# Down products of an encoder block by Strassen's scheme over pairs of token blocks, their stationary operands made beside the gate and up products; gate by SiLU

## The chip, the cores and the metric

The kernel runs on one core of a Trainium2 chip. The metric is device time in microseconds (us); all times here are of that core. The core has a matrix engine (TensorE, PE in the profile), a vector engine (VectorE, DVE), an activation engine (ScalarE, ACT), a general engine (GpSimd, POOL) and a sequencer that here only issues transfers (SyncE, SP). Each engine works through its own list of instructions in order and waits on semaphores for the others.

## The reference

One layer of an encoder on 2048 tokens of width 1024, in float32: a mixer (gated linear attention in both directions and a gated spatial mixing), then the feed-forward part, which is what matters here:

```python
x = x + concat(y_a, y_b) @ w_out
h2 = rmsnorm(x, norm2_g)
x = x + (silu(h2 @ w_gate) * (h2 @ w_up)) @ w_down    # d_ff = 2816
return rmsnorm(x, final_norm_g)
```

## The kernel before

Everything is kept with channels on the 128 partitions and tokens along the free dimension. The 2048 tokens are four blocks of 512 (`NB`, `TB`); a tile of 128 channels by 512 tokens of a block is the unit of work, 1024 channels are eight such tiles (`KT`), the 2816 channels of the feed-forward part are 22 (`NF`). Each float32 operand is split in two, a high part rounded by ScalarE (a cast) and the rest, by a subtraction on VectorE, and a product is three matmuls of 128x128 by 128x512: high by high, high by low, low by high (`mm_pass3`, L109 to L112).

Before the feed-forward part come the mixer's projections, attention, gating and the product with `w_out`. The normalised inputs of the feed-forward part and the residual wait in DRAM (`d_h`, `d_x`).

**Gate and up** (`seven`, `gate_set`, `up_set`, from L866) already use Strassen's scheme in Winograd's form. A pair of blocks, first (3, 2), then (1, 0), by the two halves of the 1024 input channels is a 2x2 matrix of moving operands, two tiles of output channels by two halves of inputs is the stationary one, and seven products of 12 matmuls stand for the eight. `moving` (L232) makes the seven moving operands of a pair in SBUF (`slots`). `Stationary.job` (L328) makes the seven stationary ones of each set just ahead of their use, on VectorE and ScalarE, from weights loaded on SP, up to four products ahead. For each pair there are 11 sets for gate and 11 for up, taken in the order `STEADY` = 0, 4, 3, 1, 2, 6, 5 within a set. Two products share a bank of PSUM with another: product 4 adds to what product 0 left, and so must wait until ScalarE has copied that out (`u2`); product 6 adds to product 3's after VectorE has read it. A quarter of a gate set then goes through tanh on ScalarE (L946) and a multiply-add on VectorE (L947); a quarter of an up set is multiplied by it (L958) and written to DRAM by POOL (`d_a`, L959).

**Down** (from L983) has no such scheme. The four blocks go one after the other in the order 3, 2, 1, 0. For each of the 22 input tiles the activation is loaded from DRAM (`act_unit`, L1014) and split, 128 rows of `w_down` are loaded (`down_unit`, L1001) and split, and eight products of three matmuls add into eight banks of PSUM. At a block's end the eight results are added to the residual (L1075), squared, summed over the partitions by a matmul with ones, and the block is normalised (`leave`, L1028) and written out by POOL while the next block's products run. Only the last block's last four input tiles are done in two halves of 256 tokens, so that the first half is normalised under the second's matmuls (L1080 to L1128).

The order on every engine comes from the framework's scheduler, which lists instructions by its own estimate of when each can start; buffers in pools (`bufs`) and semaphores decide the rest. Transfers that SP issues go in order too: one that waits holds those behind it.

## Time and profile before

| | us |
|---|---|
| median of 3 runs | 2127.7 (2124.53 to 2128.52) |
| the profiled execution's own time | 2127.53 |
| its span, first to last instruction | 2125.8 |
| mean granted TensorE clock | 0.998 of full speed |
| PE, DVE, ACT, POOL busy | 2088.7, 1362.1, 871.8, 169.3 |
| first gate matmul, first down matmul, last down matmul start | 778.48, 1628.43, 2115.08 |

The profile is of one execution. Busy times say how long an engine had an instruction in work; a matmul is pipelined, so its listed 0.39 us overlaps with the next, which starts 0.227 us later. On VectorE too the listed durations overlap by a little when nothing waits. In the views below a name such as `pd` is a tile (the bank of a down product), `out<-in` says what an instruction writes and reads, and `L110` is a line of the program.

### The profile page before, as it was taken

What the parts mean: (1) busy time and instruction counts of PE and PEld (TensorE: products, weight loads), DVE (VectorE), ACT (ScalarE), POOL (GpSimd) and SP (SyncE); (2) the same over time, 40 slices, a digit from 0 to 9 for tenths busy, and PEclk for the clock granted to TensorE, in tenths of its full rate; (3) what the DMA queues carried; (4) which work ended last, traced back from release to release, by engine and by line L of the source; (5) the groups of instructions that cost most, each with busy time, mean ns of one, the idle gap of its engine ahead of it and who ended that gap; (6) DMA issues with size and microseconds to landing.
All of it is one profiled execution on the core that took longest, in us unless ns stands there. A gap on an engine that the chain in (4) does not pass through costs nothing.

```text
span 2125.8 us, 25829 instructions
## 1 busy us (share of the span) xinstructions
PE 2088.7 (98%) x9728; PEld 1705.8 (80%) x9728; DVE 1362.1 (64%) x2134; ACT 871.8 (41%) x1475; POOL 169.3 (8%) x266
## 2 busy tenths in 40 slices
PE   8999999999999999999999999999999999999998
PEld 6777777888888878888888888888888888888887
DVE  4977666666756768676666976666666455353633
ACT  5855455464635543332332523323324333233321
POOL 0112213011110100000000000000000000000000
PEclk9999999999999999999999999999999999999999
DMA  7543225353553433222212342222225537364531
GB/s 262 199 142 120 98 96 184 133 199 125 170 187 127 169 129 144 84 70 85 95 66 83 126 149 83 69 85 95 79 72 185 185 121 257 128 216 149 180 114 40
DMA packets 94110, 281.42 MB, mean 132 GB/s; under 512 B 11681, under 2 KB 19745, under 8 KB 90785
## 3 DMA queue, kind: packets, MB, share of 16 engines
q1 hardware_dynamic: 79968, 227.33, 31.5%
q0 software_dynamic: 14016, 52.44, 6.7%
q8 instruction: 76, 1.25, 0.2%
q14 instruction: 50, 0.40, 0.1%
HBM read 225.20 MB, written 54.53 MB: 132 GB/s over the span
## 4 chain that ended last, share of the span: by engine, by line
PE 88%; DVE 5%; ACT 3%; DMA 3%; issue 1%; SPq 0%; POOL 0%; DVEq 0%; ACTq 0%; POOLq 0%
PE pd L110 8%; PE pd L111 8%; PE pd L112 8%; PE pout L112 3%; PE pout L111 3%; PE pout L110 3%; PE pu L110 1%; PE pu L111 1%; PE pu L112 1%; PE pz L110 1%; PE pz L111 1%; PE pg L110 1%; PE pg L111 1%; PE pz L112 1%; PE pg L112 1%
## 5 line engine op out<-in xcount | busy, mean ns | idle before, releaser
L959 POOL DMA_DIRECT2D da<-q x88 | 47.6, 541 | 803.1 <-DVE q L958 770.3
L946 ACT ACTIVATE th<-cg 128x512 f32<-128x512 f32 x66 | 41.5, 631 | 107.9 <-DVE cg L944 99.5
L947 DVE SCALAR_TENSOR_TENSOR cg<-th,cg 128x512 f32<-128x512 f32 x66 | 45.3, 688 | 15.6 <-ACT th L946 15.6
L826 DVE TENSOR_TENSOR xc<-pout,xc 128x512 f32<-128x512 f32 x32 | 21.9, 688 | 45.0 <-PE pout L112 44.9
L958 DVE SCALAR_TENSOR_TENSOR q<-q,cg 128x512 f32<-128x512 f32 x66 | 45.3, 687 | 0.6
L541 POOL TENSOR_SCALAR qs<-QK,misc 128x128 f32<-128x128 f32 x30 | 24.9, 833 | 164.5 <-PE po L545 83.6
L1031 POOL DMA_DIRECT2D out_dram<-xg x12 | 8.6, 716 | 368.3 <-DVE xg L1028 368.3
L565 DVE SCALAR_TENSOR_TENSOR sf<-sf,misc,dsb 64x128 f32<-64x128 f32 x56 | 19.8, 354 | 23.9 <-ACT dsb L555 23.2
L731 DVE SCALAR_TENSOR_TENSOR sb<-sb,misc,dsr 128x128 f32<-128x128 f32 x30 | 9.9, 345 | 33.8 <-PE pob L721 33.0
L548 ACT COPY ot<-po 128x256 f32<-128x256 f32 x32 | 10.3, 376 | 46.1 <-issue 23.4
L536 PEld LDWEIGHTS po<-v,s 128*128 128x128 f32 x128 | 15.5, 191 | 16.1 <-issue 13.8
L536 PE MATMUL po<-v,s 128*128 128x128 f32 x128 | 18.1, 284 | 9.9 <-DVE s L513 9.9
L1016 ACT CAST a_8h<-ar 128x512 fp32r<-128x512 f32 x32 | 18.5, 618 | 17.8 <-DMA ar<-da 17.7
L716 POOL TENSOR_SCALAR qb<-qb,misc 128x128 f32<-128x128 f32 x30 | 18.9, 640 | 78.1 <-DMA qb<-dq 66.5
L1103 DVE TENSOR_TENSOR xg<-pd,xg 128x256 f32<-128x256 f32 x16 | 6.8, 424 | 28.2 <-PE pd L112 27.8
L1075 DVE TENSOR_TENSOR xg<-pd,xg 128x512 f32<-128x512 f32 x24 | 16.6, 690 | 12.2 <-PE pd L112 12.2
L1105 ACT ACTIVATE lsq<-xg 128x256 f32<-128x256 f32 x16 | 6.7, 417 | 40.9 <-DVE xg L1103 40.9
L735 ACT ACTIVATE junk<-o 128x128 f32<-128x128 f32 x64 | 19.8, 310 | 8.8 <-DMA o<-do 4.4
L375 ACT ACTIVATE xk<-xk 128x1024 f32<-128x1024 f32 x16 | 17.0, 1063 | 13.8 <-DMA xk<-in_xtok_dram 13.8
L1017 DVE TENSOR_TENSOR a_0l<-ar,a_0h 128x512 fp32r<-128x512 f32 x32 | 20.6, 686 | 1.0 <-ACT a_0h L1016 1.0
L1017 DVE TENSOR_TENSOR a_8l<-ar,a_8h 128x512 fp32r<-128x512 f32 x32 | 20.7, 681 | 0.6 <-ACT a_8h L1016 0.6
L507 PEld LDWEIGHTS sc<-QK 64*128 64x128 f32 x256 | 15.6, 187 | 6.5 <-issue 5.3
(3680 smaller groups left out, 7337.0 us busy)
## 6 DMA issues: line engine op xcount, KB each, us to landing
wdn<-in_wdn_dram SPq DMA_DIRECT2D x88, 512.0 KB, 3.5
da<-q POOLq DMA_DIRECT2D x88, 256.0 KB, 2.3
ar<-da SPq DMA_DIRECT2D x88, 256.0 KB, 4.1
wo<-in_wo_dram SPq DMA_DIRECT2D x32, 512.0 KB, 3.6
wqk<-in_wqk_dram SPq DMA_DIRECT2D x16, 512.0 KB, 3.7
xk<-in_xtok_dram SPq DMA_DIRECT2D x16, 512.0 KB, 5.1
wv<-in_wv_dram SPq DMA_DIRECT2D x16, 512.0 KB, 3.4
xc<-in_xT_dram SPq DMA_DIRECT2D x4, 2048.0 KB, 9.2
```

What stands on the lines that cost most here:

```text
L110: nc.tensor.matmul(out=out, lhsT=whi, rhs=ahi, start=start, stop=False, **kw)
L111: nc.tensor.matmul(out=out, lhsT=whi, rhs=alo, start=False, stop=False, **kw)
L112: nc.tensor.matmul(out=out, lhsT=wlo, rhs=ahi, start=False, stop=stop, **kw)
L536: nc.tensor.matmul(out=po[hd % 2][:, hd // 2, :], lhsT=s[:, hd, :], rhs=vs[t][:, hd, :], start=hd < 2, stop=g == 0 and hd > 1)
L541: nc.gpsimd.tensor_scalar_mul(qs[:, m, :], qd[m][:, c], ech[:, m, 2 * g:2 * g + 1])
L565: nc.vector.scalar_tensor_tensor(out=sn[r, m, :], in0=sf[r, m, :], scalar=dec[r, m, g:g + 1], in1=dsb[r, 2 * m + a, :], op0=ALU.mult, op1= ...
L826: nc.vector.tensor_tensor(out=xt[:, n, :], in0=p, in1=xt[:, n, :], op=ALU.add)
L946: nc.scalar.activation(out=th, in_=a, func=AF.Tanh, scale=0.5)
L947: later.append(lambda: nc.vector.scalar_tensor_tensor(out=o, in0=th, scalar=1.0, in1=a, op0=ALU.add, op1=ALU.mult))
L958: nc.vector.scalar_tensor_tensor(out=q, in0=a, scalar=0.5, in1=cg[:, 2 * m + t, :], op0=ALU.mult, op1=ALU.mult)
L959: nc.gpsimd.dma_start(out=d_a[pair[t]][2 * p + m], in_=q)
L1017: nc.vector.tensor_tensor(out=lo, in0=raw, in1=hi.bitcast(F32), op=ALU.subtract)
```

## The change

- **Down by seven products.** For a pair of blocks the input channels are cut in three parts of eight, eight and six tiles, that is, halves of four, four and three tiles (`PARTS`). In each part four sets `q` of two output tiles each are seven products of 12 matmuls (9 in the last part). Per pair 4 sets x 7 x (12 + 12 + 9) = 924 matmuls, for both pairs 1848; before there were 2112 of that size. The function `seven` is moved out of the gate and up stage and serves both; in a part products 0 and 4 of all four sets come first, then the other five set by set (`DOWN`).
- **Stationary operands.** They do not depend on the pair, and are made once: `make_down` loads two tiles of `w_down`, makes the seven operands one after the other in one buffer of each kind, and POOL writes each high and low part to DRAM (`d_w`). There are 12 such (part, set) pieces, each spread over one set of gate and up (14 products, a step every two). In the down stage `fetched` loads them in pairs on SP, twice, once for each pair of blocks.
- **Moving operands.** `acts` loads a part's activations of both blocks, `moving` makes the seven operands; the next part's are begun within a part as its slots come free.
- **Results.** Each quarter is added to the residual in SBUF (`acc`), the last part's also squared and summed. The first pair is normalised while the second pair's first products run, and only then is the second's residual loaded over it; the second pair is normalised after its last product, whole blocks of 512 tokens.
- **Gate.** Tanh and multiply-add become one SiLU on ScalarE; the 0.5 of the up quarter goes.
- The scratch for POOL's transfer descriptors is halved, to 4096.

```diff
-        for k in range(0, HK, 2):
-            c = slice(k, k + 2)
+        for k in range(0, src.shape[1], 2):
+            c = slice(k, min(k + 2, src.shape[1]))
...
+    PARTS = (HK, HK, NF // 2 - 2 * HK)
...
+    DOWN = [(c, q, o) for c in range(len(PARTS)) for order in (STEADY[:2], STEADY[2:])
+            for q in range(KT // 2) for o in order]
+    PLACE = {x: j for j, x in enumerate(DOWN)}
+    d_w = [[drp.tile([P, D], F32, tag=f"dw{j}{x}", name=f"dw{j}{x}") for x in "hl"] for j in range(len(DOWN) // 2)]
...
+        def fetched(self, j):
+            if j % 2 == 0:
+                self.two = [wp.tile([P, D], F32, tag="w" + x, name=f"dn{self.n}{x}") for x in "hl"]
...
+                    nc.sync.dma_start(out=t, in_=d)
...
-                nc.scalar.activation(out=th, in_=a, func=AF.Tanh, scale=0.5)
-                later.append(lambda: nc.vector.scalar_tensor_tensor(
-                    out=o, in0=th, scalar=1.0, in1=a, op0=ALU.add, op1=ALU.mult))
+                nc.scalar.activation(out=o, in_=a, func=AF.Silu)
...
+        def make_down(c, q, name):
...
+            room = xp.tile([P, KT, TB], F32, tag="x2", name=name).rearrange("p k t -> p (k t)")
+            ra, rb, sm = room[:, 0:2 * w], room[:, D:D + 2 * w], room[:, 2 * D:2 * D + w]
+            hi, lo = (room[:, 2 * D + k * TB:2 * D + k * TB + w] for k in (1, 2))
...
+            for o in STEADY:
...
+                if how:
+                    src = how[0]
+                    nc.vector.tensor_tensor(out=how[0], in0=how[1], in1=how[2], op=how[3])
...
+                nc.scalar.copy(out=hi.bitcast(F32R), in_=src)
+                nc.vector.tensor_tensor(out=lo.bitcast(F32R), in0=src, in1=hi, op=ALU.subtract)
+                j = PLACE[c, q, o]
+                for x, d in zip((hi, lo), d_w[j // 2]):
+                    nc.gpsimd.dma_start(out=d[:, j % 2 * TB:j % 2 * TB + w], in_=x)
+                yield
...
+        spans = [(0, p) for p in range(3, 8)] + [(1, p) for p in range(2, 9)]
...
+            def down_set(c, q, acc=acc, square=square):
+                def quarter(m, t, a, b):
+                    def work():
+                        o = acc[q][:, 2 * t + m, :]
+                        if b is not None:
+                            add(o, b)
+                        add(o, a)
+                        if c == len(PARTS) - 1:
+                            square(m, t, q)
...
+            for c in range(len(PARTS)):
+                sets = {q: down_set(c, q) for q in range(KT // 2)}
+                mine = [(q, o) for x, q, o in DOWN if x == c]
+                for n, (q, o) in enumerate(mine):
+                    sets[q][o]()
+                    if n < 10:
+                        drain(operands, 1)
+                    elif n == 10:
+                        drain(operands)
+                        j = i * len(PARTS) + c + 1
+                        operands = acts(j % len(PARTS), PAIRS[j // len(PARTS)]) if j < 2 * len(PARTS) else None
+                    elif 16 <= n:
+                        drain(operands, 1)
...
-    nc = _bacc.Bacc("TRN2", target_bir_lowering=False, num_devices=1, dynamic_dma_scratch_size=8192)
+    nc = _bacc.Bacc("TRN2", target_bir_lowering=False, num_devices=1, dynamic_dma_scratch_size=4096)
```

Three places show the new order. First ScalarE in a set of gate and up of the second pair (channels 5), from the copy of product 0 (`u2g`) on; before, it held the splits of the next stationary operands (`op...h`) and the tanh (`th`):

```order
L913 COPY u2g_5_11291<-g_5a 128x512 [waits PE_49]
L357 CAST op230h<-wg_5b 128x512 [waits PE_49,Activation_49]
L946 ACTIVATE th_5_0_11328<-g_5a 128x512 [waits DMASW4_49,DMASW6_49,DVE_49,PE_49]
L357 CAST op230h<-wu_5a 128x512 [waits DMAHW2_49]
L357 CAST op232h<-wu_5a 128x512 [waits PE_49,Activation_49]
L357 CAST op232h<-sum_11389 128x512
L946 ACTIVATE th_5_1_11385<-cg 128x512 [waits DMASW7_49,DMASW5_49,DVE_49]
```

Now the casts of `make_down` (`mk`) stand between, and each waits for the semaphore of a write by POOL (DMASW), that of the operand made before:

```order
L917 COPY u2g_5_11455<-g_5a 128x512 [waits PE_49]
L1002 CAST mk_2_12064<-mk_2_12064 128x384 [waits DMASW7_49,DMAHW1_49,DMASW1_49,Activation_49]
L381 CAST op230h<-wg_5b 128x512 [waits PE_49]
L966 ACTIVATE cg<-g_5a 128x512 [waits PE_49]
L381 CAST op230h<-wu_5a 128x512 [waits DMAHW6_49]
L1002 CAST mk_2_12064<-mk_2_12064 128x384 [waits DMASW4_49,DVE_49]
L381 CAST op232h<-wu_5a 128x512 [waits PE_49]
L381 CAST op232h<-sum_11555 128x512
L1002 CAST mk_2_12064<-mk_2_12064 128x384 [waits DMASW6_49,DVE_49]
L966 ACTIVATE cg<-cg 128x512 [waits DVE_49]
```

Second, VectorE where one group of blocks ends and the next runs. Before, at the end of block 3, the reciprocals and the normalisation of its eight tiles (`xg`) stood among splits for block 2 (`a_8l`, `wdn_..l`):

```order
L196 RECIPROCAL r_13831<-r_13831 128x128 [waits Activation_49]
L196 RECIPROCAL r_13831<-r_13831 128x128 x3
L1017 TENSOR_TENSOR a_8l<-ar_11_14067,a_8h 128x512 [waits DMAHW1_49,Activation_49]
L1028 SCALAR_TENSOR_TENSOR xg_12940<-xg_12940,gfs,r_13831 128x512 [waits DVE_49]
L1028 SCALAR_TENSOR_TENSOR xg_12940<-xg_12940,gfs,r_13831 128x512 x7
L1017 TENSOR_TENSOR a_8l<-ar_12_14101,a_8h 128x512 [waits DMAHW2_49,Activation_49]
```

Now, at the end of the first pair, the last rows of its normalisation are followed by the second pair's first quarters (`d_0_0a` is set 0's bank of product 0), each of which waits for a residual load (DMAHW) that follows a write of results (DMASW):

```order
L1109 SCALAR_TENSOR_TENSOR acc_3_13236<-acc_3_13236,gfs,tot_14267 128x512 x2
L1109 SCALAR_TENSOR_TENSOR acc_3_13236<-acc_3_13236,gfs,tot_14413 128x512 x2
L230 TENSOR_TENSOR s5l<-ac_0_14415,s5h 128x1024 [waits Activation_49]
L1077 TENSOR_TENSOR acc_0_14811<-d_0_0a,acc_0_14811 128x512 [waits DMASW1_49,DMAHW1_49,DMASW0_49,PE_49]
L1077 TENSOR_TENSOR acc_1_14834<-d_0_1a,acc_1_14834 128x512 [waits DMASW3_49,DMAHW3_49,DMASW2_49,PE_49]
L913 TENSOR_TENSOR u2d<-d_0_0b,u2d 128x512 [waits PE_49]
L230 TENSOR_TENSOR s5l<-ac_0_14415,s5h 128x1024 [waits Activation_49]
L1077 TENSOR_TENSOR acc_2_14862<-d_0_2a,acc_2_14862 128x512 [waits DMAHW5_49,DMASW5_49,DMASW4_49]
L913 TENSOR_TENSOR vvd<-d_0_0d,u2d 128x512 [waits DVE_49,PE_49]
...
L1077 TENSOR_TENSOR acc_3_14884<-d_0_3a,acc_3_14884 128x512 [waits DMAHW7_49,DMASW7_49,DMASW6_49]
L1077 TENSOR_TENSOR acc_0_14811<-d_0_0c,acc_0_14811 128x512 [waits DVE_49]
```

The row `acc_0<-d_0_0c` reads product 3's bank, to which product 6 adds next; it now stands behind the wait for the last residual. Third, the end of VectorE's list. Before, the last matmul is followed by one add, two reciprocals and eight half tiles:

```order
L1103 TENSOR_TENSOR xg_15396<-pd_7_15529,xg_15396 128x256 [waits PE_49]
L1095 RECIPROCAL rl<-rl 128x128 [waits Activation_49]
L1095 RECIPROCAL rl<-rl 128x128
L1085 SCALAR_TENSOR_TENSOR xg_15396<-xg_15396,gfs,rl 128x256 [waits DVE_49]
L1085 SCALAR_TENSOR_TENSOR xg_15396<-xg_15396,gfs,rl 128x256 x7
```

Now the sums (`tot`) of both blocks, eight reciprocals and sixteen whole tiles come after it:

```order
L1077 TENSOR_TENSOR acc_3_14884<-d_2_3c,acc_3_14884 128x512 [waits PE_49]
L1077 TENSOR_TENSOR tot_15925<-sq_3_0_16163,tot_15925 128x512 [waits Activation_49]
L1077 TENSOR_TENSOR tot_15779<-sq_3_1_16178,tot_15779 128x512 [waits Activation_49]
L1104 RECIPROCAL tot_15779<-tot_15779 128x128 [waits Activation_49]
L1104 RECIPROCAL tot_15779<-tot_15779 128x128 x3
L1104 RECIPROCAL tot_15925<-tot_15925 128x128 [waits Activation_49]
L1104 RECIPROCAL tot_15925<-tot_15925 128x128 x3
L1109 SCALAR_TENSOR_TENSOR acc_0_14811<-acc_0_14811,gfs,tot_15779 128x512 [waits DVE_49]
...
L1109 SCALAR_TENSOR_TENSOR acc_3_14884<-acc_3_14884,gfs,tot_15925 128x512 x2
```

The normalisation of one half block after the last matmul has become that of two whole blocks.

## Rows read from the trace of the kernel before

**Rows 1.** The page, busy time of each engine.

```profile
PE 2088.7 (98%) x9728; PEld 1705.8 (80%) x9728; DVE 1362.1 (64%) x2134; ACT 871.8 (41%) x1475; POOL 169.3 (8%) x266
```

**Rows 2.** Busy time by stretch: gate and up, two pieces of it, down, start.

```profile
core 0: us, PE busy (x) PEld busy (x) DVE busy (x) ACT busy (x) POOL busy (x), PEclk, DMA share, GB/s
778.48:1628.43 849.95, 847.66 (x3699) 688.87 (x3698) 608.85 (x936) 285.99 (x477) 47.57 (x88) 1.00 0.27 96
1066.00:1104.00 38.00, 38.00 (x167) 30.70 (x166) 24.62 (x40) 11.55 (x20) 2.16 (x4) 1.00 0.23 83
1180.00:1218.00 38.00, 38.00 (x169) 31.45 (x168) 37.59 (x49) 19.84 (x29) 1.64 (x3) 1.00 0.34 122
1628.43:2088.09 459.66, 459.66 (x2023) 379.52 (x2022) 211.18 (x249) 152.86 (x194) 9.13 (x13) 1.00 0.49 166
0.00:100.00 100.00, 86.68 (x373) 65.79 (x373) 68.22 (x127) 72.36 (x131) 9.78 (x25) 0.98 0.70 239
```

**Rows 3.** Timeline of TensorE: first, first half-width and last down matmuls (start, length).

```profile
1628.43 0.39 PE L110 MATMUL pd<-a_0h,wdn_0h 128*128 128x512 f32 x1
...
2088.09 0.28 PE L110 MATMUL pd<-a_16h,wdn_18h 128*128 128x256 f32 x1
...
2115.08 0.28 PE L112 MATMUL pd<-a_16h,wdn_21l 128*128 128x256 f32 x1
```

**Rows 4.** Timeline of VectorE behind the last matmul.

```profile
2115.40 0.42 DVE L1103 TENSOR_TENSOR xg<-pd,xg 128x256 f32<-128x256 f32 x1 [1.59 <-PE pd L112]
...
2119.37 3.25 DVE L1085 SCALAR_TENSOR_TENSOR xg<-xg,gfs,rl 128x256 f32<-128x256 f32 x8
```

**Rows 5.** Timelines at block 3's end: sum over partitions, reciprocals, normalisation.

```profile
1753.56 1.02 PE L193 MATMUL f3m<-acc,ones 128*128 128x512 f32 x2
...
1757.28 3.39 DVE L196 RECIPROCAL r<-r 128x128 f32<-128x128 f32 x4 [0.78 <-ACT r L194]
...
1761.13 5.38 DVE L1028 SCALAR_TENSOR_TENSOR xg<-xg,gfs,r 128x512 f32<-128x512 f32 x8
```

**Rows 6.** Transfers by kind: size, median us from issue to landing.

```profile
wdn<-in_wdn_dram SPq DMA_DIRECT2D x88, 512.0 KB, 3.5
da<-q POOLq DMA_DIRECT2D x88, 256.0 KB, 2.3
...
out_dram<-xg POOLq DMA_DIRECT2D x12, 512.0 KB, 4.2
```

**Rows 7.** The same, of the first 100 us alone.

```profile
wqk<-in_wqk_dram SPq DMA_DIRECT2D x8, 512.0 KB, 5.4
...
dq<-QK POOLq DMA_DIRECT2D x2, 256.0 KB, 5.4
```

**Rows 8.** Timeline of TensorE in a gate set, before product 6.

```profile
1413.31 0.39 PE L903 MATMUL g_5e<-s5l,op230h 128*128 128x512 f32 x1
1413.59 0.50 PE L902 MATMUL g_5c<-s6h,op228h 128*128 128x512 f32 x1
1413.93 0.40 PE L903 MATMUL g_5c<-s5l,op228h 128*128 128x512 f32 x1
```

**Rows 9.** Timeline of VectorE in that set.

```profile
1411.65 0.69 DVE L909 TENSOR_TENSOR vvg<-g_5d,u2g 128x512 f32<-128x512 f32 x1
1412.25 0.68 DVE L339 TENSOR_TENSOR sum<-sum,wu_5a 128x512 f32<-128x512 f32 x1
```

**Rows 10.** The costliest groups of the page: POOL's issue, the gate's tanh and multiply-add.

```profile
L959 POOL DMA_DIRECT2D da<-q x88 | 47.6, 541 | 803.1 <-DVE q L958 770.3
L946 ACT ACTIVATE th<-cg 128x512 f32<-128x512 f32 x66 | 41.5, 631 | 107.9 <-DVE cg L944 99.5
L947 DVE SCALAR_TENSOR_TENSOR cg<-th,cg 128x512 f32<-128x512 f32 x66 | 45.3, 688 | 15.6 <-ACT th L946 15.6
```

**Rows 11.** Groups by line, shapes apart: a split and a cast of 1024 columns.

```profile
L229 DVE TENSOR_TENSOR tbl<-xf,tbh 128x1024 fp32r<-128x1024 f32 x8 | 9.7, 1219 | 0.4 <-ACT tbh L228 0.4
L228 ACT CAST tbh<-xf 128x1024 fp32r<-128x1024 f32 x8 | 8.4, 1046 | 6.2 <-PE pout L112 4.1 <-PE u_10c L904 2.2
```

More of the change, by code (lines that the diff above doesn't have):

```diff
@@ L236, in sub @@
         def sub(o, a, b):
[L237 to L238 removed]
+            for k in range(0, o.shape[1], 2):
+                c = slice(k, min(k + 2, o.shape[1]))
                 nc.vector.tensor_tensor(out=o[:, c, :], in0=a[:, c, :], in1=b[:, c, :], op=ALU.subtract)
@@ L864, in norm_x0, with seven, product, add @@
             yield
+    first_bank = [True]
+    def seven(quarter, name, temp, hk=HK):
+        bank = {}
+        def product(i, key, start=True):
+            whi, wlo = ws.next()
+            if start:
+                bank[key] = (other(f"{name}{key}") if first_bank.pop() else None) if first_bank else None
+                if bank[key] is None:
+                    bank[key] = psf.tile([P, TB], F32, tag="sp", name=f"{name}{key}", bufs=7)
+            o = bank[key]
+            thi, tlo = slots[i]
+            for k in range(hk):
+                c = slice(k * P, (k + 1) * P)
+                f, l = start and k == 0, k == hk - 1
+                nc.tensor.matmul(out=o, lhsT=whi[:, c], rhs=thi[:, k, :], start=f, stop=False, skip_group_check=True)
+                nc.tensor.matmul(out=o, lhsT=whi[:, c], rhs=tlo[:, k, :], start=False, stop=False, skip_group_check=True)
+                nc.tensor.matmul(out=o, lhsT=wlo[:, c], rhs=thi[:, k, :], start=False, stop=l, skip_group_check=True)
+            return o
+        def add(o, a, b):
+            nc.vector.tensor_tensor(out=o, in0=a, in1=b, op=ALU.add)
+        def s0():
+            st["u2"] = temp("u2", 4)
+            nc.scalar.copy(out=st["u2"], in_=product(0, "a"))
+        def s1():
+            add(st["u2"], product(1, "b"), st["u2"])
+        def s2():
+            d = product(2, "d")
+            st["vv"] = temp("vv", 2)
+            add(st["vv"], d, st["u2"])
+            quarter(1, 1, bank["c"], st["vv"])
+        def s3():
+            product(3, "c")
+        def s4():
+            quarter(0, 0, product(4, "a", False), None)
+        def s5():
+            quarter(1, 0, product(5, "e"), st["vv"])
+        def s6():
+            quarter(0, 1, product(6, "c", False), st["u2"])
+        st = {}
+        return dict(enumerate((s0, s1, s2, s3, s4, s5, s6)))
     psums.close()
@@ L941, in quarter @@
                 o = cg[:, 2 * m + t, :]
-                th = pf.tile([P, TB], F32, tag="q", name=f"th{pair[t]}_{p}_{m}", bufs=2)
                 if b is not None:
@@ L963, in encoder_block, with acts @@
+        def acts(c, pair):
+            hk, both = PARTS[c], []
+            for b, tag in zip(pair, ("x2", "x")):
+                t = xp.tile([P, KT, TB], F32, tag=tag, name=f"ac{b}_{c}")
+                for k in (0, hk):
+                    nc.sync.dma_start(out=t[:, k:k + hk, :], in_=d_a[b][c][:, k:k + hk, :])
+                both.append(t)
+            return moving(*(t[:, k:k + hk, :] for t in both for k in (0, hk)))
         ws = ops.stream
@@ L984, in encoder_block @@
                 drain(operands, 1)
                 done += 1
-            flush()
+            elif i == 1 and p == 9 and (w, o) == (0, STEADY[0]):
+                operands = acts(0, PAIRS[0])
+            elif n > last[1] + 1:
+                drain(operands, 1)
     with tc.tile_pool(name="pg", bufs=1) as pg:
-        order = PAIRS[0] + PAIRS[1]
-        count = [0, 0]
-        def scratch(name):
-            return pg.tile([P, TB], F32, tag="sq", name=name, bufs=2)
-        def down_unit(b, j):
-            i = count[0]
-            count[0] += 1
-            pool, tag, bufs = (wp, "w", None) if i % 8 < 3 else (pg, "dw", 5)
-            raw = wp.tile([P, D], F32, tag="wraw", name=f"wdn{b}_{j}", bufs=2)
-            nc.sync.dma_start(out=raw, in_=wdn[j])
-            return split(pool, raw, [P, D], tag, f"wdn{b}_{j}", bufs)
@@ L1020, in encoder_block @@
-        group = {}
-        ws = Stream([lambda b=b, j=j: (act_unit(b, j), down_unit(b, j)) for b in order for j in range(NF)], ahead=3)
-        def leave(b, xt, sums):
-            r = pg.tile([P, TB], F32, tag="r", name=f"r{b}", bufs=1)
-            sums.rstd(r)
-            yield
-            for n in range(KT):
-                nc.vector.scalar_tensor_tensor(out=xt[:, n, :], in0=xt[:, n, :], scalar=gfs[:, n:n + 1], in1=r,
-                                               op0=ALU.mult, op1=ALU.mult)
-                if n % 2:
-                    nc.gpsimd.dma_start(out=ov[:, n - 1:n + 1, b * TB:(b + 1) * TB], in_=xt[:, n - 1:n + 1, :])
-                yield
@@ L1175, in _arrange @@
         wgu=wgu,
-        wdn=f["w_down"][0].reshape(NF, P, D),
+        wds=np.stack([stat(f["w_down"][0][c * D:(c + 1) * D]) for c in range(2)]),
+        wdt=stat(f["w_down"][0][2 * D:]),
     )
```

283 lines of the change are left out of this document (120 added, 163 removed).

## The prediction

> **What bounds the kernel now.** I read the page's busy line first, then the windows by stage, then timelines at the places that the change touches.
>
> TensorE is busy for 2088.7 of 2125.8 us [rows 1], and in the two stages that matter it is busy without a break at full clock: 847.66 of 849.95 us in gate and up, all of 459.66 us in down [rows 2]. So the time is the number of matmuls times their spacing plus whatever stops them. How much slack the others have is seen in two pieces of gate and up: at 1066 VectorE is busy 24.62 of 38 us, at 1180 it is busy 37.59 of 38 us, and TensorE has no gap in either [rows 2]. Operands are made far enough ahead that a nearly full VectorE does no harm, for a stretch that short. The transfer engines are the other resource: their share is 0.49 in down at 166 GB/s, and the highest row is 0.70 at 239 GB/s at the start [rows 2].
>
> The sum is made against the profiled execution, 2127.53 us (span 2125.8 and 1.7 around it), 0.2 under the median of the runs.
>
> **A. Matmuls of down.** Before, the 2016 whole matmuls and three blocks' sums fill 459.66 us [rows 2], 0.228 each; from the first matmul to the last one's start are 2115.08 - 1628.43 = 486.65 us [rows 3]. After, there are 1848 whole ones: 1848 x 0.228 = 421.3. That is -65.3 us. This term is firm, since TensorE does nothing else here and its clock row is 1.00 [rows 2].
>
> **B. The end.** Before, from the last matmul's start (2115.08) to the span's end are 10.7 us, with eight half tiles of normalisation ending at 2119.37 + 3.25 = 2122.62 [rows 3, 4]. After, two whole blocks hang behind the last matmul, on VectorE for the most part: 0.4 until the last add can start; the add 0.69 [rows 9], the square about 0.63 as ScalarE's tanh [rows 10], the add to the sum 0.69; the matmul over partitions 1.02 and 0.78 for the root [rows 5]; eight reciprocals, 2 x 3.39, and sixteen whole tiles, 2 x 5.38 [rows 5]; a last write of 512 KB, 4.2 [rows 6]; some 0.4 of hand-overs. Together 26.4, so +15.7. Nothing covers it: no matmul is left. The write before took 3.2 after the last tile, so the error is about 2 us.
>
> A and B alone give 2127.5 - 49.6 = 2078. The rest is what may stop TensorE in between.
>
> **C. Banks shared within a set.** The down stage takes over the order of gate and up, where product 6 waits for VectorE's read of product 3's bank: around 1413 two matmuls start 0.28 and 0.34 us after the one before them instead of 0.23 [rows 8], just where VectorE reads product 3 (`vvg<-g_5d`) and then takes its next 0.60 later [rows 9]. Over the stage: 849.95 us less 3696 matmuls at 0.2267 leaves 12.2 us for 44 sets, 0.27 each. Down has 24 sets, so +6.6. Both ends: nothing, as VectorE has less to do in down; or 1 us a set, +24, if ScalarE's copy of product 0 and VectorE's adds stand behind 1024-wide splits (1219 ns, 1046 ns [rows 11]). I take the measured one.
>
> **D. Between the pairs.** When the first pair's last product ends (call it T), VectorE has a backlog of the next moving operands and adds, six 1024-wide ones and four of 0.6, about 9 us; then eight reciprocals (6.8) and sixteen tiles (10.8) [rows 5] with two splits among them (2.4): the last tile is done at about T + 29. Its write lands 4.2 to 5 later, and only then does the residual load into the same room start, 3.5 [rows 6]: T + 38.5. VectorE's list has all four residual adds ahead of `acc_0<-d_0_0c`, which frees product 3's bank for product 6: T + 40. TensorE reaches product 6 of set 0 after 126 matmuls and two sums, T + 31. So +8 or 9; I take +8. Bounds: 0, if the backlog is small; +20, if write and load take 5.4 each as at the start [rows 7] and the backlog doubles. Behind the waiting add stand `u2d` and `vvd` of the same set, and for those TensorE waits.
>
> **E. Loads of down.** Per pair of blocks all stationary operands come from DRAM again: 40.4 MB twice, activations 23.1, residual 8.4, results 8.4: 120.6 MB in 421 us, 286 GB/s. Before it was 166 [rows 2]. Scaled by its share, the start's row gives 239 / 0.70 = 341 GB/s at full load [rows 2], so the engines would be 84% taken. A pair of operands is asked for two pairs ahead (three buffers): 2 x 24 x 0.228 = 10.9 us, 8.2 in the last part, against a landing of 3.5 in down and 5.4 under the heaviest load [rows 6, 7]. So they come in time; on SP they stand in line with activation loads and, at the start and between the pairs, with residual loads that wait. I take +2 for it, between 0 and what the rival below gives.
>
> **F. `make_down` beside gate and up.** The 12 pieces add per piece seven casts on ScalarE, eleven operations on VectorE (seven subtractions, four sums) and fourteen writes on POOL; four multiply-adds go. VectorE: 24.62 + 11 x 0.60 - 4 x 0.60 = 28.8 of 38 us [rows 2, 9]; ScalarE 11.55 + 7 x 0.63 = 16 of 38 [rows 2, 10]. Both hide under the matmuls. SiLU is not in the trace; its nearest row is the tanh, 0.63 [rows 10], and ScalarE could bear the double. The multiply-add that goes was hidden too: nothing won. What is new is a loop: a step's cast and subtraction may start only when POOL's write of the step before has landed, and behind the waiting cast stand on ScalarE the casts for the next products. Cast 0.63 + issue 0.54 [rows 10] + landing 2.3 [rows 6] = 3.5 us, and a step comes every two products, 5.5 us: it fits. I take +4 for small collisions over 462 us, between -5 (the lighter gate) and +98 (below).
>
> Sum: -65.3 + 15.7 + 6.6 + 8 + 2 + 4 = -29.0: **2098 us**.
>
> **Rivals.** (1) *The covers hold everywhere*: C to F come to nothing, 2078. For it: TensorE without a gap at 99% VectorE. Against it: the residual in D stands in one chain with long rows. 18%.
>
> (2) *VectorE loses its lead*: between 1180 and 1218 it already was full [rows 2]; with the pieces in such stretches, and splits of 1024 columns in down, C is 0.7 a set in 24 sets (+17) and F +10: 2115. 13%.
>
> (3) *The loads bind down.* If the transfers sustain only what the highest row sustained, 239 GB/s [rows 2], 120.6 MB take 505 us where the matmuls take 421: +83 in the place of E, about 2179, slower than before. It decides from some 267 GB/s downward, where the stage is 31 us longer and the gain is gone. For it: no row of the trace is above 239. Against it: that row stands at a share of 0.70, with no sign that it was the limit. 8%. On this the Trainium skill ("DMA: Bandwidth & Descriptors", section "Specifications") has a limit of about 358 GB/s from memory for one core; by it the 120.6 MB take 337 us, an estimate, and the loads hide; the trace has no row that high.
>
> (4) *The write loop binds gate and up.* Where POOL's writes stand among loads they take longer: 5.4 us in the first 100 us [rows 7]. A piece's fourteen writes of 256 KB and 1 MB of loads are 4.7 MB in 38.5 us, so the traffic there grows from 83 GB/s [rows 2] to some 206. Then a step is 0.63 + 0.54 + 5.4 = 6.6 us, seven are 46 against 38.5 of matmuls in that piece, twelve pieces cost some 95 us: about 2190, slower. It decides from a landing of about 4.7 us on. Against it: the stage's median is 2.3 at 96 GB/s [rows 2, 6]. 7%. The Trainium skill (same page, "Queues, rings and completion order") says that a transfer's semaphore signal lands only after every earlier write of the same transfer engine, across queues, so that POOL's small writes would wait for loads issued before them; the 5.4 against 2.3 agrees with it without proving it.
>
> My forecast case has 54%, and its own range is 2086 to 2110.
>
> **How the numbers follow.** A measurement of this kernel tells about 0.2% (4.3 us) from no change, so "same" is 2123.4 to 2132. Cases at 2098, 2078 and 2115 are faster, 85%, together with 2% of milder forms of (3) and (4); the rest of those two is 10% slower and 3% in between. The range goes from 2074 (case 1 less the error of B) to 2135 (D and C at their upper bounds, or a mild form of 3 or 4), leaving out some 15%.
>
> **What would show it.** Right: 1848 down matmuls in some 435 to 445 us, one gap of about 8 us behind the first pair, at product 6 of its first set; some 26 us from the last matmul to the end; gate and up within a few us of 850. Wrong: TensorE's waits in down that end with a `dn` load (3); ScalarE's casts `mk` ending waits on a POOL write of over 4.7 us with TensorE behind them (4); many short waits on VectorE in every set (2); no gap between the pairs (1). The forecast falls if gate and up grow by over 20 us or down takes over 460.

## The result: slower, and the profile after

The changed kernel takes 2155.2 us (median of 4 runs, 2147.4 to 2162.3); the ratio to before is 1.0129, 95% interval 1.0099 to 1.0159. The forecast was 2098 us, faster. The profiled execution took 2147.37, 19.8 more than the one of before. The page's busy line, to be read against [rows 1]:

```profile
PE 2042.8 (95%) x9352; PEld 1648.7 (77%) x9352; DVE 1474.3 (69%) x2302; ACT 865.6 (40%) x1483; POOL 257.6 (12%) x430
```

TensorE has 46 us less to do, and yet ends later. The windows say where, to be read against [rows 2]: gate and up, a piece of it without `make_down` and one with it, down, and the place between the pairs:

```profile
core 0: us, PE busy (x) PEld busy (x) DVE busy (x) ACT busy (x) POOL busy (x), PEclk, DMA share, GB/s
774.44:1659.67 885.23, 855.53 (x3699) 692.15 (x3698) 639.30 (x987) 336.64 (x563) 138.48 (x256) 0.99 0.41 148
1066.00:1104.00 38.00, 38.00 (x167) 30.70 (x166) 22.25 (x36) 11.45 (x20) 2.15 (x4) 1.00 0.23 82
1300.00:1338.00 38.00, 35.46 (x154) 28.27 (x153) 26.07 (x44) 14.92 (x26) 9.74 (x19) 1.00 0.53 195
1659.67:2118.33 458.66, 432.92 (x1853) 346.81 (x1851) 293.64 (x383) 101.05 (x129) 6.29 (x9) 0.97 0.67 242
...
1920.00:1940.00 20.00, 7.18 (x17) 4.77 (x18) 7.40 (x11) 0.00 (x0) 0.00 (x0) 0.57 1.01 400
```

The bounds are matmul starts, so the stages add up: the mixer ends 4.0 us earlier, gate and up are 35.3 longer (885.2 against 850.0), down from first to last start 28.0 shorter (458.7 against 486.7), the end 16.6 longer (27.3 against 10.7). Together that is 19.9; the spans differ by 19.8. In gate and up the same 38 us lose nothing where no piece is made and 2.5 where one is, with VectorE at 26 of 38: not full, but late.

### The profile page after: what moved, and what is told of

It reads as the page before. It is cut to its first block, busy times and chain, and to the rows that moved or that the text cites. A ratio compares the mean times of both kernels' runs of the same rounds, so it can differ in the third digit from the quotient of the medians.

```text
span 2145.7 us, 25554 instructions
## 1 busy us (share of the span) xinstructions
PE 2042.8 (95%) x9352; PEld 1648.7 (77%) x9352; DVE 1474.3 (69%) x2302; ACT 865.6 (40%) x1483; POOL 257.6 (12%) x430
## 4 chain that ended last, share of the span: by engine, by line
PE 53%; issue 26%; DVE 8%; POOL 6%; DMA 4%; ACT 3%; SPq 0%; POOLq 0%; DVEq 0%; ACTq 0%
PE pout L112 3%; PE pout L113 3%; PE pout L111 3%; POOL da L978 2%; PE pu L111 1%; PE pu L112 1%; PE pu L113 1%; PE pz L111 1%; PE pz L112 1%; PE pz L113 1%; PE pg L111 1%; PE pg L112 1%; PE pg L113 1%; PE pqk L112 1%; PE po L560 1%
## 5 line engine op out<-in xcount | busy, mean ns | idle before, releaser
L1002 ACT CAST mk<-mk 128x512 fp32r<-128x512 f32 (+1 forms) x84 | 49.1, 585 | 142.3 <-DVE mk L999 24.4
L1003 DVE TENSOR_TENSOR mk<-mk 128x512 fp32r<-128x512 f32 (+1 forms) x84 | 54.0, 643 | 75.7 <-ACT mk L1002 16.4
L229 ACT CAST tbh<-ac 128x1024 fp32r<-128x1024 f32 (+1 forms) x24 | 23.1, 978 | 154.8 <-issue 82.5
L966 ACT ACTIVATE cg<-cg 128x512 f32<-128x512 f32 x66 | 41.5, 630 | 74.2 <-DVE cg L964 74.1
L976 DVE TENSOR_TENSOR q<-q,cg 128x512 f32<-128x512 f32 x66 | 45.1, 685 | 0.4
L230 DVE TENSOR_TENSOR tbl<-ac,tbh 128x1024 fp32r<-128x1024 f32 (+1 forms) x24 | 26.8, 1128 | 7.1 <-ACT tbh L229 7.1
L1077 DVE TENSOR_TENSOR acc<-vvd,acc 128x512 f32<-128x512 f32 x48 | 31.0, 686 | 0.5
L999 DVE TENSOR_TENSOR mk<-mk 128x512 f32<-128x512 f32 (+1 forms) x48 | 30.8, 642 | 0.6
L230 DVE TENSOR_TENSOR tal<-ac,tah 128x1024 fp32r<-128x1024 f32 (+1 forms) x24 | 26.8, 1130 | 2.3 <-ACT tah L229 2.3
L240 DVE TENSOR_TENSOR ac<-ac 128x1024 f32<-128x1024 f32 (+1 forms) x24 | 26.9, 1127 | 1.4 <-DMA ac<-da 1.4
L560 PEld LDWEIGHTS po<-v,s 128*128 128x128 f32 x128 | 15.5, 191 | 14.7 <-issue 12.4
```

The lines of the kernel that those rows point to most:

```text
L229: nc.scalar.copy(out=hi[:, c, :], in_=src[:, c, :])
L230: nc.vector.tensor_tensor(out=lo[:, c, :], in0=src[:, c, :], in1=hi[:, c, :].bitcast(F32), op=ALU.subtract)
L560: nc.tensor.matmul(out=po[hd % 2][:, hd // 2, :], lhsT=s[:, hd, :], rhs=vs[t][:, hd, :], start=hd < 2, stop=g == 0 and hd > 1)
L966: nc.scalar.activation(out=o, in_=a, func=AF.Silu)
L976: nc.vector.tensor_tensor(out=q, in0=a, in1=cg[:, 2 * m + t, :], op=ALU.mult)
L1002: nc.scalar.copy(out=hi.bitcast(F32R), in_=src)
```

## Where the time goes in the two stages

**Gate and up.** TensorE's waits between 800 and 1600 (last numbers: us in total, times, longest) are many and short, and end mostly with VectorE's read of product 3's bank (`cg`, `q`), which product 6 needs; the others, such as the last line, wait for ScalarE's copy of product 0 (`u2`):

```profile
PE u_4c L907 <- DVE q L974: 5.3, 2, 3.1
PE g_6c L907 <- DVE cg L964: 3.2, 1, 3.2
PE u_1c L907 <- DVE q L974: 2.7, 1, 2.7
PE u_2c L907 <- DVE q L974: 2.3, 2, 1.5
PE g_3a L907 <- ACT u2g L917: 2.2, 1, 2.2
```

Summed over the stage the stops of more than 0.4 us are 33.5 us, before 2.0. What VectorE does ahead of the 3.1 us stop at 1417 (timelines of VectorE, then of POOL):

```profile
1405.54 0.56 DVE L1003 TENSOR_TENSOR mk<-mk 128x384 fp32r<-128x384 f32 x1 [2.74 <-DMA dw34l<-mk]
...
1411.51 0.55 DVE L1003 TENSOR_TENSOR mk<-mk 128x384 fp32r<-128x384 f32 x1
1411.97 0.68 DVE L913 TENSOR_TENSOR u2u<-u_4b,u2u 128x512 f32<-128x512 f32 x1
1414.61 0.56 DVE L1003 TENSOR_TENSOR mk<-mk 128x384 fp32r<-128x384 f32 x1 [1.95 <-DMA dw35l<-mk]
1415.08 0.68 DVE L913 TENSOR_TENSOR vvu<-u_4d,u2u 128x512 f32<-128x512 f32 x1
...
1416.28 0.68 DVE L974 TENSOR_TENSOR q<-u_4c,vvu 128x512 f32<-128x512 f32 x1
```

```profile
1412.35 0.54 POOL L1006 DMA_DIRECT2D dw35l<-mk  x1 [2.38 <-DVE mk L1003]
```

The write issued at 1412.35 has landed at 1414.61, 2.3 us later: no slow write. But the next step's subtraction already stands two instructions behind the one before it, and behind it the adds that TensorE waits for.

**Down.** The chain between the pairs is the predicted one, row by row, only later (VectorE; the first pair's last product ends at 1888):

```profile
1897.47 6.62 DVE L1104 RECIPROCAL tot<-tot 128x128 f32<-128x128 f32 x8
...
1914.14 2.73 DVE L1109 SCALAR_TENSOR_TENSOR acc<-acc,gfs,tot 128x512 f32<-128x512 f32 x4
1916.80 1.22 DVE L230 TENSOR_TENSOR s5l<-ac,s5h 128x1024 fp32r<-128x1024 f32 x1
1922.43 0.69 DVE L1077 TENSOR_TENSOR acc<-d_0a,acc 128x512 f32<-128x512 f32 x1 [4.42 <-DMA acc<-dx]
1927.43 0.69 DVE L1077 TENSOR_TENSOR acc<-d_1a,acc 128x512 f32<-128x512 f32 x1 [4.32 <-DMA acc<-dx]
...
1934.50 0.68 DVE L1077 TENSOR_TENSOR acc<-d_0c,acc 128x512 f32<-128x512 f32 x1
```

The last tile is done at T + 29, as forecast; `acc_0<-d_0_0c` comes at T + 46, not T + 40. The transfers of down show why (KB each, median us to landing):

```profile
ac<-da SPq DMA_DIRECT2D x12, 1024.0 KB, 9.1
acc<-dx SPq DMA_DIRECT2D x16, 512.0 KB, 7.1
...
out_dram<-acc POOLq DMA_DIRECT2D x8, 512.0 KB, 9.5
```

The results take 9.5 us instead of 4.2 [rows 6] and the residual 7.1 instead of 3.5, while results, residual and operands share transfer engines that are full, at 400 GB/s. TensorE stops three times, 15.7 us together, and its granted clock is 0.57 over these 20 us, the lower of its two levels (1.2 GHz) for 17 of them. Its other waits in down:

```profile
PE d_3a L907 <- DMA dn314h<-dw3h: 4.1, 1, 4.1
...
PE d_2e L909 <- DMA dn386l<-dw39l: 1.5, 1, 1.5
PE d_0e L907 <- DMA dn376h<-dw34h: 1.3, 1, 1.3
```

The first is the start: on SP eight residual loads took from 1662.3 to 1671.4 to issue, and the operands behind them landed 9.7 us after their own issue. A granted clock of 0.83 for the 20 us from 1680 on followed. Five late operands between 1833 and 1885 cost another 5.4.

## The experiments

All are variants of the changed kernel; "gu" is gate and up, "down" from the first to the last start there, "tail" from that to the end of the span, each from the run's one profiled execution, which in nowrite and best5 took 10 us less than the run's median.

| kernel | median us | ratio to before (95%) | gu | down | tail |
|---|---|---|---|---|---|
| before | 2127.7 | | 850.0 | 486.7 | 10.7 |
| changed | 2155.2 | 1.0129 (1.0099 to 1.0159) | 885.2 | 458.7 | 27.3 |
| dbl | 2151.5 | 1.0113 (1.0082 to 1.0143) | 883.7 | 459.5 | 27.3 |
| nowrite | 2126.9 | 0.9992 (0.9982 to 1.0002) | 857.1 | 456.3 | 27.5 |
| nomake | 2123.5 | 0.9978 (0.9966 to 0.9990) | 855.1 | 457.1 | 27.4 |
| switch | 2155.3 | 1.0124 (1.0103 to 1.0145) | 891.1 | 457.7 | 28.2 |
| paced | 2135.5 | 1.0042 (1.0027 to 1.0056) | 869.7 | 458.8 | 28.2 |
| paced2 | 2140.5 | 1.0060 (1.0042 to 1.0079) | 869.5 | 459.0 | 27.3 |
| paced_nw | 2116.5 | 0.9943 (0.9929 to 0.9956) | 849.0 | 459.4 | 28.2 |
| early | 2137.9 | 1.0042 (1.0027 to 1.0056) | 869.8 | 458.9 | 28.2 |
| deep | 2132.2 | 1.0015 (1.0005 to 1.0025) | 864.2 | 458.5 | 27.3 |
| start | 2153.0 | 1.0114 (1.0093 to 1.0134) | 888.3 | 455.2 | 28.2 |
| lateres | 2153.6 | 1.0110 (1.0079 to 1.0141) | 891.5 | 453.7 | 29.1 |
| best1 | 2138.5 | 1.0051 (1.0032 to 1.0070) | 872.3 | 458.8 | 29.5 |
| best2 | 2129.8 | 1.0006 (0.9990 to 1.0021) | 870.4 | 449.5 | 29.1 |
| best3 | 2130.8 | 1.0016 (1.0003 to 1.0030) | 875.9 | 451.3 | 27.5 |
| best4 | 2129.8 | 1.0008 (0.9993 to 1.0024) | 870.2 | 451.2 | 27.4 |
| best5 | 2131.5 | 1.0020 (1.0006 to 1.0034) | 867.9 | 451.0 | 25.6 |
| best6 | 2123.9 | 0.9974 (0.9964 to 0.9984) | 864.6 | 453.6 | 25.2 |
| best7 | 2123.6 | 0.9974 (0.9960 to 0.9987) | 867.9 | 453.2 | 25.3 |

### What the 35 us of `make_down` are

**dbl**, a second pair of buffers:

```diff
+            twos = [[room[:, 2 * D + k * TB:2 * D + k * TB + w] for k in (1, 2)],
+                    [room[:, 2 * D + 3 * TB:2 * D + 3 * TB + w], extra[:, 0:w]]]
...
+                hi, lo = twos[step % 2]
```

> The changed kernel with a second pair of buffers for the high and low parts in make_down, used by turns; nothing else moves. Theory (waits): gate and up are 35 us longer because a step's cast and subtraction wait until the write of the step before has landed, and VectorE and ScalarE stand in order behind that wait; with two pairs that wait is gone, gate and up fall from 885 to 855 to 862 us, the time to 2125 to 2132, and TensorE's waits on cg and q shrink to under 5 us. Rival (work): the eleven VectorE and seven ScalarE instructions themselves push the adds of a set back: gate and up stay at 880 or more, the time at 2150. Rival (traffic): the writes slow the weight loads: stays as well.

Nothing was won, though the casts' and subtractions' waits for their own writes fell from 112 us to 44: the theory as it stood fell. VectorE, then ScalarE, at one of its stops:

```profile
1349.60 0.56 DVE L1006 TENSOR_TENSOR mk<-mk 128x384 fp32r<-128x384 f32 x1 [5.10 <-ACT mk L1005]
1350.08 0.55 DVE L1006 TENSOR_TENSOR mk_1x<-mk 128x384 fp32r<-128x384 f32 x1
```

```profile
1349.05 0.93 ACT L1005 CAST mk<-mk 128x384 fp32r<-128x384 f32 x2 [4.78 <-DMA mk<-in_wdt_dram]
```

Two steps now stand side by side, and the first waits for the piece's own weights: with more room the scheduler put the steps still closer together (casts 2.3 us apart in the median, in the changed kernel 4.4) and earlier: a piece's first cast runs 64 to 143 us ahead of the gate set that the program makes it beside, in the changed kernel 58 to 89.

**nowrite** and **nomake**:

```diff
+                for x, d in zip((hi, lo), d_w[j // 2]) if (c, q) == (0, 0) else ():
     nc.gpsimd.dma_start(...)
...
+        spans = [(0, 3)]          # nomake instead
```

> make_down does all its casts, sums and subtractions, but only the first of the twelve pieces is written; down loads the same operands again and again (so down's result is not the reference's), with as many loads of the same size. Theory (waits): gate and up 855 to 860, time about 2127, like two buffers. Rival (work): 880 or more, 2150. Rival (traffic): gate and up 855 here, but 880 with two buffers.

> Only the first of the twelve pieces of make_down is made at all; down loads that piece's operands again and again (its result is not the reference's). The floor for gate and up with SiLU: all theories 849 to 853 us, time about 2118 with down as it is (459 us and a tail of 27). What lies between this and the run without writes is the price of the work, between that and the changed kernel the price of writing.

Without the writes 28 of the 35 us go, without the work as well another 2. The work is nearly free, the writes are the price. nomake stayed above its forecast of 849 to 853, so it is not the floor: the one piece that both runs still make and write costs TensorE a stop of 3 us by itself. Whether the price is paid through the waits on the writes or through their traffic, these two don't tell.

**paced**, the order alone:

```diff
+                last = [next(x for x in reversed(traced) if x.engine == e) for e in (DVE, ACT)]
+                with tc.issue_after(last[0]), tc.issue_after(last[1]):
                     ...   # sum, cast, subtraction and writes of a step, as they were
```

> The changed kernel with make_down's instructions, one buffer of each kind as there, tied in VectorE's and ScalarE's lists behind the instruction that was written just before them, so that a step really stands every two products; traffic, buffers and work are the same. Theory (bunching): the scheduler had put the steps of a piece close together at its head, so that every step waits for the landing of the step before, and a second pair of buffers only made it bunch more. Spread out, the wait ends before a step begins: gate and up 855 to 862 us instead of 885, time 2125 to 2132. Rival (traffic): the 40 MB of writes themselves slow the loads of gate and up's weights: gate and up stay at 878 or more, time 2148 or more.

15.5 of the 35 us go with work, buffers and bytes the same, so those are the order's; it is less than expected, and a rest of 20 is left. Bunching is only a part of what pacing took away: the casts now start 5.1 us apart in the median instead of 4.4, and a piece's first cast 8 to 17 us after the start of its gate set instead of 58 to 89 ahead of it. **paced2** and **paced_nw** (that with `dbl`, and that with `nowrite`'s line):

> The paced steps together with the second pair of buffers. Theory (waits on landing): what was left of gate and up's loss with pacing alone (870 us against 857 without writes) was still the wait of a step for the write before, now two steps old when it is waited for: gate and up 856 to 860, time 2125. Rival (traffic or head of line on POOL): what is left is not the wait for one's own buffer but other things: gate and up stay at 868 or more, time 2135.

> Paced steps, and only the first of the twelve pieces is written to DRAM (down loads that piece's operands again and again, its result is not the reference's). Pacing with writes left gate and up at 870 us, the unpaced kernel without writes at 857. Theory (head of a piece): the rest is the wait of a piece's first cast for its own weights, loaded two products earlier, and hence there without writes too: 865 or more. Rival (traffic): the writes make weight loads land late: 854 to 858.

paced_nw, at 849.0, lies under both forecasts and 1 us under the kernel before, so the rest is not the work: 20 us come with the writes. (Taken in the other order, the writes are worth 28 us and pacing without them 8.) Two pairs of buffers leave the rest whole, so it isn't the wait of a cast or subtraction for its own buffer. The windows of the two runs over the stage, paced, then paced_nw (columns as above):

```profile
775.17:1644.90 869.73, 851.65 (x3699) 690.16 (x3698) 640.69 (x987) 336.59 (x563) 138.46 (x256) 1.00 0.42 151
```

```profile
779.03:1628.07 849.04, 846.30 (x3699) 689.66 (x3698) 639.72 (x987) 337.31 (x563) 55.17 (x102) 1.00 0.31 111
```

The traffic differs by 40 GB/s. Summed between 860 and 1600, the casts and subtractions of `make_down` wait for their own writes 112 us in the changed kernel, 57 paced, 1 in paced2. In that order VectorE's waits for gate and up's weights (`sum` from `wg`, `wu`) grow: 34, 34, 54; in paced_nw they are 14. But those waits alone don't stop TensorE: in the kernel before they are 34 us too and in nomake 54, and in neither does TensorE wait between 860 and 1600. VectorE in paced2 ahead of a stop of 2.7 us, weights first, then the piece's own:

```profile
1381.05 0.69 DVE L363 TENSOR_TENSOR sum<-wg_5b 128x512 f32<-128x512 f32 x1 [2.92 <-DMA wg_5b<-in_wgu_dram]
...
1385.76 0.69 DVE L1011 TENSOR_TENSOR mk<-mk 128x512 fp32r<-128x512 f32 x1 [2.21 <-ACT mk L1010]
```

The second wait is the one that is new at this place; eight of the thirteen stops from 950 on have it ahead of them. It has a cause that the two forecasts leave out. All pieces use one room (`x2`, a single buffer), and the second pair of buffers lies for the most part in it, so SP may load the next piece's weights only when the last write of the piece before has landed. POOL's last write and SP's load in paced2:

```profile
1375.47 0.54 POOL L1014 DMA_DIRECT2D dw25l<-mk  x1
```

```profile
1378.88 0.80 SPq L995 DMA_DIRECT2D mk<-in_wds_dram  x2
```

That write lands at 1378.75. In paced_nw the load follows the last subtraction, with no write to wait for (VectorE, then SP):

```profile
1364.97 0.69 DVE L1008 TENSOR_TENSOR mk<-mk 128x512 fp32r<-128x512 f32 x1 [0.69 <-ACT mk L1007]
```

```profile
1365.69 0.81 SPq L993 DMA_DIRECT2D mk<-in_wds_dram  x2
```

Over nine pieces (all that directly follow another, except the one behind the piece that paced_nw does write) the first load is issued 6.3 us after the start of its gate set in paced_nw and 9.6 in paced2, and lands at 9.9 and 14.3. So 3.3 of the 4.4 us are the wait for the landing of the last write, 1.1 a longer flight. The lists differ as well: in paced_nw the weights of the piece stand ahead of `wg_5b` on SP, and VectorE takes `sum<-wg_5b` four instructions later.

**early** (with two pairs), **deep** (with one) go at these loads:

```diff
-                elif turn % 2 == 0:
+                elif turn in (1, 4, 6, 8, 10, 12, 13):          # early
...
-                while ... (self.asked[x] < 2 or q[self.asked[x] - 2]["last"] < done):
+                deep = 2 + x                                     # deep; 3 - x in best7
+                while ... (self.asked[x] < deep or q[self.asked[x] - deep]["last"] < done):
```

> Paced steps with two pairs of buffers, and a piece's weights are loaded one product earlier, its last two steps one product apart instead of together. Theory (head of a piece): the first cast's wait of 2 to 3.6 us at each piece's start goes, and the gaps at product 6 of the piece's gate set with it: gate and up 862 to 865 instead of 869.5, time 2133. Rival (traffic): 868 or more.

> Paced steps, one pair of buffers, and one of the two queues of gate and up's weights three tiles deep instead of two, so that its loads are issued one set earlier (the room is taken from the four copies of product 0, now three). Theory (late weight loads): with pacing but no writes VectorE waits 10 us for the second half of the weights in gate and up, with the writes 28 to 41, and that is what is left of the loss: gate and up 858 to 862 instead of 870, time 2125. Rival (one's own write): the remaining wait of casts for the write before (43 us on ScalarE) is what counts, or both: 867 or more, 2134.

early won nothing, for the piece's weights were not loaded earlier: on SP they waited for the last write as before, and were issued 10.0 us after the start of the gate set. deep brought 5.5 us, but not by its theory: the longer queue was that of the up weights, and VectorE still waits 42 us for gate and up's weights. **best7** lengthens the gate's queue, with two pairs of buffers and best6's edits in down (below):

> Paced steps with two pairs of buffers, the queue of the gate's weights three tiles deep (in deep it was the up's), and the edits of best6 in down. In paced2 the casts and subtractions wait 1 us in all for their own writes, VectorE 54 us for gate and up's weights (14 without the writes), and every stop of TensorE but none other follows such a wait of 2.2 to 3.6 us for wg or wu. Theory (late gate weights): with the gate's loads a set earlier these waits fall under 25 us and gate and up to 852 to 858 us instead of 869.5; with down 451 and tail 25 the time is about 2110, faster than before by 0.8%. Rival (bandwidth, whatever the queue's depth): waits stay over 40 and gate and up at 866 or more, time 2124.

The waits for weights fall to 21 us, the gate's from 41 to 5, and still the stage takes 867.9: the theory fell as to the price. Ten of its eleven stops between 950 and 1600 now follow a wait for a piece's first cast, that is, for its own weights (VectorE, then ScalarE, ahead of a stop of 3.2 us):

```profile
1383.25 0.69 DVE L1012 TENSOR_TENSOR mk<-mk 128x512 fp32r<-128x512 f32 x1 [3.24 <-ACT mk L1011]
```

```profile
1382.60 0.62 ACT L1011 CAST mk<-mk 128x512 fp32r<-128x512 f32 x1 [4.30 <-DMA mk<-in_wds_dram]
```

In best7 too these weights are issued 9.6 us after the start of the gate set and land at 14.3. So it is shown that the writes cost some 20 us of gate and up even when paced, and that the stops follow the piece's own weights, not the gate's. That the wait for the last write's landing makes them late, more than the traffic, is read from the traces; a second room for the pieces, which would tell the two apart, wasn't run, nor the writes with the list of paced_nw.

### What the stops in down are

**start** (residual loads behind products 2 to 5), **switch** (activations six products later) and **lateres** (second pair's residual added in the last part):

```diff
-                for q in range(KT // 2):
-                    residual(q)
+                later = [lambda q=q: residual(q) for q in range(KT // 2)]     # start
...
+                    late = 6 if (i, c) == (1, 0) else 0                      # switch
+                    if n == 10 + late:
                         operands = acts(...)
...
+                if pair == PAIRS[-1]:                                        # lateres
+                    return
```

> The changed kernel, but the first pair's residual is loaded after products 2 to 5 of down instead of ahead of the first, so that those eight transfers no longer stand on SP before the operands dn314. Theory: TensorE's stop of 4.3 us at 1681 and the low clock behind it (0.83 for 20 us, some 3 us) go: down 451 us instead of 459, time 2147. Rival: the operands then come late at another product, since the same bytes flow: down 456 or more, time 2153.

> The changed kernel, but in the second pair's first part the next part's activations (4 MB) are loaded six products later. Theory (bandwidth at the switch): between 1895 and 1935 result writes, residual loads, operands and activations are some 19 MB at over 400 GB/s, writes take 9.5 us and residual loads 7; with the activations later writes take 5 to 6, and TensorE's stop between the pairs falls from 16 to about 8 us, time 2145. Rival (chain): the chain of reciprocals, normalisation, write and load is long by itself: the stop stays at 14 or more, time 2153.

> The changed kernel, but the second pair's first quarters are put into the cleared room without the residual, which is loaded and added in the last part. So they wait for the landing of the first pair's results alone and not for a load behind it. Theory (chain): of the 16 us stop between the pairs the 7 us of the load go, and the queue on SP with them: stop 6 to 9, time about 2147. Rival (VectorE): reciprocals and normalisation alone reach to 1917, 7 us before TensorE wants the bank, and the writes of 9.5 us behind them are enough to hold it: stop stays at 13 or more, time 2153.

start: the stop of 4.3 us at `dn314` is gone, one of 3.3 at the first set's adds has come 25 us later; 3.5 us of down are won, between the two forecasts. switch: the edit moved only one of the four transfers of 1 MB. Counted from the 924th matmul of down they were issued after 14, 14, 46 and 46 us in the changed kernel and after 14, 14, 45 and 60 here. So the three stops of 15.6 us, as before, don't tell whether activations lengthen the chain. lateres: four short stops, 6.6 us, stand where 15.7 were, as the chain's theory expected (VectorE in that run):

```profile
1926.03 0.68 DVE L1123 COPY acc<-d_0a 128x512 f32<-128x512 f32 x1
...
1934.75 0.69 DVE L1123 COPY acc<-d_2a 128x512 f32<-128x512 f32 x1 [4.34 <-DMA out_dram<-acc]
...
1941.09 0.69 DVE L1123 COPY acc<-d_3a 128x512 f32<-128x512 f32 x1 [5.05 <-DMA out_dram<-acc]
```

VectorE now waits for the results' landing alone, and down is 5 us shorter. As gate and up varied by as much between runs (885 to 891 with its code the same), these two show in the stage and not in the medians.

### All together

**best1** is paced, start, lateres and the reciprocals on 4 columns; **best2** has two pairs of buffers and the old reciprocals; **best3** is best2 with the root by exp and ln in one bank, **best4** that with the activations of switch; **best5** is best2 with early and the root by exp and ln in two banks; **best6** is best5 with deep in place of the second pair and of early, best7 is told above. The root's edit:

```diff
-                nc.scalar.activation(out=total[t], in_=m, func=AF.Sqrt, bias=eps, scale=1.0 / D)
-                    nc.vector.reciprocal(...)
+                nc.scalar.activation(out=total[t], in_=m, func=AF.Ln, bias=eps, scale=1.0 / D)
+                            nc.scalar.activation(out=total[x], in_=total[x], func=AF.Exp, scale=-0.5)
```

> Paced steps, residual loads spread at the start, late residual of the second pair, and the reciprocals taken on 4 columns of tokens-on-partitions and spread again by a matmul with ones (8 reciprocals of 128 columns less per pair). If the three stops are separate their gains add: 2155 less 26 (pacing), 7 (start), 7 (residual) and 5 each at the end and between the pairs: about 2107, faster than before. If waits only move on, 2125 or more.

> Paced steps with two pairs of buffers, spread residual loads at the start and the late residual of the second pair, with the reciprocals as they were. If the stops are separate: gate and up 857, down 449, tail 28: about 2115, faster than before by 0.6%. If the freed transfers only collide elsewhere in down: 455 or more and 2122.

> That, with the spread residual loads, the late residual of the second pair and exp(-0.5 ln x) for the root, the two blocks' sums in two banks: gate and up 864, down 450, tail 24: about 2118, faster than before by 0.5%. If each freed wait is taken up by the next: 2126.

> The same with the spread residual loads, the late residual of the second pair and exp(-0.5 ln x) for the root in two banks: gate and up 860, down 450, tail 25: about 2112, faster than before by 0.7%. If gate and up stay at 868 as in the last combination: 2124.

The gains add in part. best1's reciprocals only moved the wait: behind the last matmul the sums went back and forth between TensorE, ScalarE and VectorE, and the tail grew to 29.5. best2 and best4 equal before, and best3 is 0.16% slower; its tail of 27.5 missed the forecast of 23 to 25. In best5 to best7 earlier results between the pairs wait longer for their landing, one stop of 8 us, so down gained nothing by them; the tail fell by 2 to 3. best6 and best7 are faster than before by 0.26% (0.16 to 0.36% and 0.13 to 0.40%): they beat the kernel before by 5 us, where A and B alone promised 50.

## Why the prediction was wrong, step by step

- **A, matmuls (-65.3), and B, the end (+15.7)**: right. 1848 matmuls stand in down; the end cost 16.6. Nothing of the error is here but 1 us.
- **F, `make_down` (+4; measured +35.3)**: the step that failed. "A step comes every two products, 5.5 us: it fits" took the program's order for the order on the engines. The steps stand in the lists of VectorE and ScalarE where the scheduler's estimate put them, a piece 58 to 89 us ahead of its gate set and its casts 4.4 us apart in the median, so a landing of 2.3 us, which the sum had as harmless, stood in front of the adds for product 6. paced shows 15.5 of it. Another 20 come with the writes also when paced (869.5 in paced2 against 849.0 in paced_nw). The sum let a step wait for the write of the step before, but had no term for the next piece's weights, which wait for the last write into the one room and land 4.4 us later than without writes; how much of the 20 that is, and how much traffic and another list, stays open. Rival 4 had the loop, but with a threshold of 4.7 us landing and a wait on ScalarE alone; it needed no slow write. What the trace showed was rival 2's mark, many short waits on VectorE, in most of the sets with a piece.
- **D, between the pairs (+8; measured +15.7)**: mechanism right, size wrong. Its two landings were taken from a quieter stretch; with results, residual and operands at 400 GB/s they were 9.5 and 7.1. Both lie beyond the 5.4 of its upper bound. (Its own parts add up to T + 37.5 at most, not to T + 38.5.) lateres shows the chain.
- **E, loads (+2; measured 9.7)**: 4.3 at the start and 5.4 on late operands; the forecast saw the queue on SP and gave it too little.
- **C (+6.6; measured 12.0)**: what of down's 37.4 us over 1848 x 0.228 belongs neither to D nor to E: 3.2 in short stops and 8.8 in wider spacing, the low clock behind the stops among it. So most of it is not the wait that C names.
- **Rival 3** (239 GB/s) is refuted: full transfer engines moved 400 GB/s, above both limits that it names, and down's mean of 242 left them at 0.67. That no row of before is above 239 was misread: the page of before has slices of 262 and 257.

The excess is 31.3 in F, 7.7 in D, 7.7 in E, 5.4 in C and 0.9 in B, less 4.0 of the mixer, which no term has: the 49 us between forecast and profiled execution. The median lies another 8 above that.

## What to carry to other kernels

Where a scheduler sets the order, read on the engine's list, not in the program, where and how far apart the steps of a background task stand: a wait that fits between two steps by the program may stand in front of the critical adds. A background task that writes is not free: price it by the run that leaves its writes out, and then look for every instruction that waits for their landing, among them the loads that reuse the room they read. A run that leaves something out can also change the lists, and an edit that moves a transfer in the program need not move it on its queue; read both from the trace. And a landing time from a quiet stretch is a lower bound for the same transfer where several megabytes move at once.

## What was not expected of the hardware

The transfers reached 400 GB/s over 20 us (share 1.01), where the row of before that the forecast went by, 239 at 0.70, let one expect 341. And a stop of a few us costs more than itself: the granted clock was 0.83 between 1680 and 1700, at the end of a stop of 4.3 us, the lower level (1.2 GHz) for 6.6 of these us.
